# Low parts of weights on VectorE, mixing between the gates' pairs, LayerNorm as paced work: a change to a two-branch decoder kernel

## The chip, the core and the metric

The kernel runs on one core of one Trainium2 chip. The metric is the device time of one execution in microseconds (us). TensorE multiplies (PE in the rows, its weight loads PEld), VectorE (DVE) and ScalarE (ACT) do elementwise work, GpSimd (POOL) issues the accumulating DMAs, SyncE (SP) issues most loads and stores.

## The reference, cut to what matters

One layer over 1040 prompt positions (16 learned ones ahead of 1024) and 64 sample positions (8 sequences of 8, with states), D = 1024, all float32:

```
h = rmsnorm(x); z = h @ w_in            # seven column groups of 1024
u = a_val * sigmoid(a_gate)             # GLU
c = causal_depthwise_conv(u, width 31) + b
c = silu(layernorm(c)) * silu(a_silu);  br_a = c @ w_conv_out
pooled = trailing_mean(p_in, 2/4/8/16 by channel group) - p_in
q = (pooled per group @ w_pool_mix) * pool_scale * silu(p_silu)
br_b = q @ w_pool_out
y = rmsnorm(x + (sigmoid(g_a)*br_a + sigmoid(g_b)*br_b) @ w_out)
```

The last 30 values of `u` and the last 15 of `p_in` are returned as new states.

## The kernel before

Channels lie on the 128 partitions, positions on the free axis, in two halves `h` of 552 columns (8 learned, 512 prompt, 32 sample) or 544 without the learned ones. Every float32 operand of a product is split into a high part (rounded to the type that TensorE takes) and a low part (the rest), and a product is three passes: high x high, high x low, low x high (`gemm`). Two helpers make the parts. `split` casts on ScalarE and subtracts on VectorE:

```python
act.copy(dst_h, src)
dve.tensor_tensor(dst_l, src, dst_h.bitcast(F32), ALU.subtract)
```

`split_dma` casts on ScalarE, writes the negated high part with `act.mul` into the low tile, and lets an accumulating DMA of GpSimd's queue add the source.

The stages, in order of emission:

1. *Plain products* of p0 to p5 (pool inputs) with x before its normalisation (`plain`, `keep_raw`), while the root of the mean square is made. Then VectorE normalises x (L332) and `split_x` makes the operands hx.
2. *Blocks*: 18 products of 96 matmuls (p6, p7, then gate g and value v of each of eight chunks of the GLU). Weights are loaded two blocks ahead and split one block ahead (`Block.split`, by default `split_dma`). A v block ends in the GLU, whose result goes to DRAM (d_e, d_es) and comes back as the convolution's input.
3. *Pairs*: 16 pairs of column blocks (q, b, a, s: the four gates), each by seven products of 24 matmuls instead of eight (`seven`), with sums of weights on VectorE and low parts mostly by `split_dma`. All gates go to DRAM.
4. *Mixing*: the pooled operand, split when it was made (`pool_work`, `out`), is loaded as two parts and multiplied by w_pool_mix, gated (L840) and split into the slots q.
5. *Branch B's projection* (`ppo`, 8 x 2 halves of 48 matmuls). Beside it, after the first half of blocks written out by hand, LayerNorm: the mean from a sum that accumulating DMAs made, the squares, the root (`inv_root`), and `branch_a`, which makes the operands cx.
6. *Branch A's projection* (`pco`, of the same size) with the merge, then the final projection (`pwo`) and norm.

VectorE's convolution (31 taps of 1024 columns per chunk and four sample steps) and the pooling are queued work: `push` puts lists of (cost, step) into `todo`, and `fill(until)` emits steps while the planner's account of VectorE stays under the one of TensorE. `step(us)` adds to TensorE's account and runs what `defer` has put off by a number of steps; `spend(n)` charges VectorE with 0.22 + n/960 us for work that is emitted outside the queue. Every engine and queue runs its instructions in the order of emission. Tiles come from rings: 35 slots of 4.4 KB a partition, ten half raw weights, six half operands, eight z tiles (half a row of positions), four PSUM tiles of two banks. A tile is given back when nothing refers to it any more, and whoever takes the next one waits for that.

Of the kernel before, what the change touches and what calls it, by code (L numbers as in the profile page):

```python
# [14 lines left out]
P = 128  # L15
# [28 lines left out]
NSLOT, NWS, NOP, NZ = 35, 10, 6, 8  # L44
# [4 lines left out]
BLOCKS = "p6 p7 " + " ".join(f"g{i} v{i}" for i in range(8))  # L49
# [19 lines left out]
def hybrid_trunk_kernel(  # L69
# [40 lines left out]
    ones32 = const.tile([P, P], F32, name="ones32")  # L110
# [67 lines left out]
    def totals(s, n, name):  # L178
        hl = [slot(f"sum{x}_{name}", (2, n), F32R) for x in "hl"]
        split(hl[0], hl[1], s)  # L180
        out = slot(f"total_{name}", (2, n))
# [149 lines left out]
    for k in range(NK):  # L331
        dve.scalar_tensor_tensor(xs[k], xs[k], col(OFF_NG, k), rms, ALU.mult, ALU.mult)  # L332
        split_x(0, (k,), split)
    plain1(1)
    plain1(2)
    keep_raw(1, 1, outs[1])
    split_x(1, (0, 1), split)
    plain1(3)
    keep_raw(2, 1, outs[2])
    split_x(1, (2, 3), split)  # L340
    plain1(4)
    keep_raw(3, 1, outs[3])
# [94 lines left out]
    def seven(w, units, put):  # L437
# [14 lines left out]
        y = bank2(f"py_{name}")  # L452
        act.copy(y[:, :, :n], x[:, :, :n])
        yield
        v = bank2(f"pv_{name}")
        product_of(v, "q3", "T3", True, False)
        yield
        fill(clock["pe"])
# [25 lines left out]
    d_gate, d_sga, d_sgb, d_sa, d_c, d_tb = (  # L484
        dram.tile([NK, P, 2, H2], F32, name=f"d_{x}") for x in ("gate", "sga", "sgb", "sa", "c", "tb")
    )
    d_pool = dram.tile([NK, P, 2, 2, H2], F32, name="d_pool")
# [14 lines left out]
    def pool_load(j):  # L502
        if j < NK:
            lraw[j] = [half(f"lraw{j}{h}") for h in range(2)]
            for h in range(2):
                sp.dma_start(out=lraw[j][h], in_=d_raw[j][:, h])

    def pool_work(j):
# [3 lines left out]
        def start():  # L512
# [3 lines left out]
            sp.dma_start(out=es[:, :, :PB], in_=spool[j])  # L516
            for h in range(2):
# [11 lines left out]
            defer(2, lambda: sp.dma_start(out=o_ps[j], in_=es[:, :, DS:]))  # L529
# [10 lines left out]
        def last():  # L540
            e, es, s, ss = cur
            dve.scalar_tensor_tensor(s[:, META:], s[:, META:], 1.0 / w, e[:, META:], ALU.mult, ALU.subtract)  # L542
            dve.scalar_tensor_tensor(ss[:, :, PB:], ss[:, :, PB:], 1.0 / w, es[:, :, PB:], ALU.mult, ALU.subtract)

        def out(h):
            s, ss = cur[2:]
            o = slot(f"poolop{j}{h}", (2, H2), F32R)
            b = slice(h * DB // 2, (h + 1) * DB // 2)
            split_dma(o[:, 0, :HP], o[:, 1, :HP], s[:, META + h * HP : META + (h + 1) * HP])
            split(v3(o[:, 0, HP:], DS), v3(o[:, 1, HP:], DS), ss[:, b, PB:])  # L550
            defer(3, lambda: sp.dma_start(out=d_pool[j][:, h], in_=o.bitcast(F32)))
# [7 lines left out]
        for h in range(2):  # L559
            work.append((0.25, lambda h=h: out(h)))  # L560
# [5 lines left out]
    def gate_pair(i, base, name, func, dst):  # L566
        def put(b, h, z):
            o = z
            if not b:
                o = half2(f"z{name}{i}{b}{h}", H2)  # L570
            act.activation(o, z, func)
            act.dma_start(out=dst[2 * i + b][:, h], in_=flat(o))

        return [(w_in[base + 2 * i], w_in[base + 2 * i + 1], f"{name}{i}", UNITS2, put)]
# [3 lines left out]
    d_e = dram.tile([NK, P, TP], F32, name="d_e")  # L578
    d_es = dram.tile([NK, P, DB, DS], F32, name="d_es")


    class Conv:
        fetched = []

        def __init__(self, i):
            self.i = i
            work = [(t_op(SEQ) if k else 0.75, lambda k=k: self.taps(k)) for k in range(CW)]
            work += [(1.5, lambda b=b: self.sample(b)) for b in range(0, DB, 2)]
# [11 lines left out]
        def fetch(self):  # L600
            i = self.i
            e = self.e = slot(f"ce{i}", (CB + TP,))
            es = self.es = st.tile([P, DB, ES], F32, tag="ces", name=f"ces{i}", bufs=2)
            pool.memset(e[:, :CB], 0.0)
            sp.dma_start(out=e[:, CB:], in_=d_e[i])
            sp.dma_start(out=es[:, :, :CB], in_=sconv[i])
            sp.dma_start(out=es[:, :, CB:], in_=d_es[i])
            defer(3, lambda: sp.dma_start(out=o_cp[i], in_=e[:, TP : TP + CB]))
            defer(3, lambda: sp.dma_start(out=o_cs[i], in_=es[:, :, DS:]))
# [28 lines left out]
        def store(self):  # L638
            Conv.fetched.remove(self)
            Conv.more()  # L640
            defer(2, self.put)

        def put(self):
            sp.dma_start(out=d_c[self.i], in_=self.c)
            if not csum:
                csum.append(dram.tile([P, 2, H2], F32, name="d_csum"))
                sp.dma_start(out=csum[0], in_=self.c)
            else:
                pool.dma_start(out=csum[0], in_=self.c, accum_op=ALU.add)
# [6 lines left out]
    def put_block(kind, i, h, ps):  # L656
# [7 lines left out]
        else:  # L664
            z = sg.pop(h)
            dve.tensor_tensor(v3(z, HT // 2), ps, v3(z, HT // 2), ALU.mult)
            spend(HT)
            m, p, s = parts4(z)

            def out():  # L670
                sp.dma_start(out=d_e[i][:, META + h * HP : META + (h + 1) * HP], in_=p)
                sp.dma_start(out=d_e[i][:, h * HM : (h + 1) * HM], in_=m)
                sp.dma_start(out=d_es[i][:, h * DB // 2 : (h + 1) * DB // 2], in_=s)

            defer(1, out)
# [6 lines left out]
    ops[0].split()  # L682
# [7 lines left out]
    def make_t(k, how):  # L690
# [13 lines left out]
        "q": lambda i: gate_pair(i, PSG, "q", AF.Silu, d_gate),  # L704
# [35 lines left out]
    pooled, wm = {}, {}  # L740

    def load_pooled(j):
        pooled[j] = [slot(f"lp{j}{h}", (2, H2), F32R) for h in range(2)]
        for h in range(2):
            sp.dma_start(out=pooled[j][h].bitcast(F32), in_=d_pool[j][:, h])

    def load_mix(g):
        raw = half_raw(f"mraw{g}")
        sp.dma_start(out=raw.rearrange("p k c -> p (k c)"), in_=w_mix[g].rearrange("p k c -> p (k c)"))
        wm[g] = op_tile(f"m{g}", (2, 2, 2 * P))  # L750
        split(wm[g][:, 0], wm[g][:, 1], raw.rearrange("p (k a) c -> p k (a c)", k=2))
# [3 lines left out]
    lgate = {}  # L755

    def load_gate(j):
        lgate[j] = [fetch_half(d_gate[j], h, f"lg{j}") for h in range(2)]

# [3 lines left out]
    for n, (kind, i) in enumerate(blocks):  # L763
# [3 lines left out]
        if n + 1 < len(blocks):  # L767
            ops[n + 1].split()
# [5 lines left out]
        for h in (0, 1) if left > 1 else (1, 0):  # L774
# [4 lines left out]
            if n == 0 and h == 0:  # L779
                keep_raw(5, 1, outs[5])  # L780
# [12 lines left out]
    clock["t"] = 0  # L793
    cur = pairs[0][1]
    next(cur), next(cur), next(cur)
    after = iter(())
    for n in range(len(pairs)):
        nxt = pairs[n + 1][1] if n + 1 < len(pairs) else None
        next(after, None)
        next(cur)  # L800
        if nxt:
            next(nxt)
        else:
            load_mix(0)
            load_gate(0)
            load_pooled(0)
            load_pooled(1)
        next(cur)
        if nxt:
            next(nxt)  # L810
        next(cur)
        if nxt:
            next(nxt)
        after, cur = cur, nxt
    next(after, None)
    fill()

    load_pooled(2)
    load_gate(1)
    q = []  # L820
    for j in range(NK):
        if j + 3 < NK:
            load_pooled(j + 3)
        if j + 2 < NK:
            load_gate(j + 2)
        if j % 2 == 0 and j < 6:
            load_mix(j // 2 + 1)
        if j == 4:
            po[0].load()
            po[0].split()  # L830
        if j == 6:
            po[1].load()
        g, i = j // 2, j % 2
        q.append([])
        for h in range(2):
            ps = gemm_half(
                f"pmix{j}", lambda k, s: wm[g][:, s, k, i * P : (i + 1) * P], [pooled[2 * g], pooled[2 * g + 1]], h, 2
            )
            z = lgate[j][h]
            dve.scalar_tensor_tensor(of_half(z), ps, col(OFF_PS, j), of_half(z), ALU.mult, ALU.mult)  # L840
            q[j].append(operand(f"q{j}{h}", z, split))
            step(1.5)


    conv = [slot(f"lc{i}", (2, H2)) for i in range(NK)]
    lcsum = slot("lcsum", (2, H2))
    sp.dma_start(out=lcsum, in_=csum[0])
    cx = []
    lsa = {}

    def load_sa(i):
        lsa[i] = [fetch_half(d_sa[i], h, f"lsa{i}") for h in range(2)]

    def branch_a(i, how):
        cx.append([])
        dve.tensor_tensor(conv[i], conv[i], rstd, ALU.mult)
        act.activation(conv[i], conv[i], AF.Silu, bias=col(OFF_LB, i), scale=col(OFF_LG, i))
        for h in range(2):
            dve.tensor_tensor(conv[i][:, h], conv[i][:, h], lsa[i][h], ALU.mult)
            cx[i].append(operand(f"cx{i}{h}", conv[i][:, h], how))  # L860

    for d in range(NK):
        (po + co)[d + 2].load()
        lb = [fetch_half(d_sgb[d], h, f"lb{d}") for h in range(2)]
        if d == 0:
            for i in range(NK):
                sp.dma_start(out=conv[i], in_=d_c[i])
        (po + co)[d + 1].split()
        if d == 1:
# [250 lines left out]
```

## Time and profile before

| | us |
|---|---|
| median of three runs (1117.55 to 1118.63) | 1117.84 |
| the profiled execution | 1117.58 |
| its span, first to last instruction | 1115.8 |
| TensorE busy | 990.3 |
| VectorE busy | 731.9 |
| ScalarE busy | 469.1 |
| GpSimd busy | 174.4 |

Busy time is that of the profiled execution. Matmuls overlap, so their durations add up to more than the time in which they run; the distance between two starts is what one costs. PEclk is the clock granted to TensorE as a share of full speed; its two levels are 2.4 and 1.2 GHz.

### The profile page before, as it was taken

To read this page: it belongs to the slowest core of one execution; us is meant where nothing else is said; L and a number is where in the kernel's file an instruction comes from. 1 tells how busy PE (TensorE), PEld (TensorE's weight loads), DVE (VectorE), ACT (ScalarE), POOL (GpSimd) and SP (SyncE) were. 2 spreads that over 40 slices of the span, in tenths; PEclk is the share of its full clock that TensorE was granted. 3 is DMA by queue.
4 is the path that set the end of the run, shared out by engine and by line. 5 is a ranking of instruction groups with operands and counts; after the bars stand their busy time and mean duration, and the time that the engine had idled before them with its cause. 6 is when DMAs were issued, how large, how long until landed. Compare 5 with 4: busy or idle time off the path is not lost. (4 is left out here: it accounts for less than half of the span.)

```text
span 1115.8 us, 18229 instructions
## 1 busy us (share of the span) xinstructions
PE 990.3 (89%) x7176; PEld 962.1 (86%) x7176; DVE 731.9 (66%) x945; ACT 469.1 (42%) x791; POOL 174.4 (16%) x211
## 2 busy tenths in 40 slices
PE   9978885789999899999999999759967649999997
PEld 9978885789999899999999999758967649998885
DVE  7473542698998999999898998354434443355333
ACT  7635432313325665655455555234236452225111
POOL 0001211111213222322222232001011121000000
PEclk9999998789999999999999999979998969999999
DMA  9217999996559797989879796999346569544222
GB/s 318 73 48 165 198 214 201 205 233 162 119 143 204 171 234 185 225 200 207 197 176 239 180 224 145 309 343 320 101 107 184 161 187 279 153 155 150 77 94 95
DMA packets 144805, 205.94 MB, mean 185 GB/s; under 512 B 59216, under 2 KB 60624, under 8 KB 144720
## 3 DMA queue, kind: packets, MB, share of 16 engines
q1 hardware_dynamic: 104832, 128.42, 38.6%
q0 software_dynamic: 28368, 54.01, 28.0%
q10 hardware_dynamic: 11520, 22.35, 6.0%
q8 instruction: 56, 0.92, 0.3%
q14 instruction: 29, 0.24, 0.1%
HBM read 99.37 MB, written 55.27 MB: 139 GB/s over the span
## 5 line engine op out<-in xcount | busy, mean ns | idle before, releaser
L621 DVE SCALAR_TENSOR_TENSOR c<-ce,pv,c 128x1024 f32<-128x1024 f32 x240 | 307.9, 1283 | 5.9
L149 PE MATMUL pv<-hx,w_v 128*128 128x276 f32 x768 | 105.1, 299 | 20.7 <-DMA w_v<-raw_v 20.7
L149 PEld LDWEIGHTS pv<-hx,w_v 128*128 128x128 f32 x768 | 103.2, 197 | 21.8 <-DMA w_v<-raw_v 21.8
L149 PE MATMUL pco<-cx,w_co 128*128 128x272 f32 x768 | 101.6, 295 | 22.4 <-DMA w_co<-raw_co 11.4
L149 PEld LDWEIGHTS pco<-cx,w_co 128*128 128x128 f32 x768 | 100.1, 194 | 23.8 <-DMA w_co<-raw_co 12.1
L149 PE MATMUL pg<-hx,w_g 128*128 128x276 f32 x768 | 104.5, 298 | 14.2 <-DMA w_g<-raw_g 14.2
L149 PEld LDWEIGHTS pg<-hx,w_g 128*128 128x128 f32 x768 | 103.0, 197 | 14.9 <-DMA w_g<-raw_g 14.9
L149 PE MATMUL ppo<-q,w_po 128*128 128x272 f32 x768 | 100.0, 293 | 6.4 <-DMA w_po<-raw_po 6.0
L149 PEld LDWEIGHTS ppo<-q,w_po 128*128 128x128 f32 x768 | 99.2, 192 | 7.2 <-DMA w_po<-raw_po 6.4
L993 PE MATMUL pwo<-wo,mx 128*128 128x512 f32 x336 | 79.3, 394 | 0.0
L993 PEld LDWEIGHTS pwo<-wo,mx 128*128 128x128 f32 x336 | 63.1, 188 | 14.8
L149 PE MATMUL pp<-xg,wh_p 128*128 128x276 f32 x384 | 66.8, 296 | 7.8 <-ACT rawp L259 7.7
L149 PEld LDWEIGHTS pp<-xg,wh_p 128*128 128x128 f32 x384 | 56.5, 194 | 8.7 <-ACT rawp L259 7.9
L149 PE MATMUL pmix<-lp,m 128*128 128x272 f32 x192 | 31.5, 329 | 16.7 <-DVE lg L840 10.6
L878 DVE TENSOR_TENSOR lb<-ppo,lb 128x544 f32<-128x544 f32 x16 | 11.5, 722 | 52.0 <-DMA lb<-d_sgb 40.2
L149 PEld LDWEIGHTS pmix<-lp,m 128*128 128x128 f32 x192 | 29.6, 225 | 18.5 <-issue 10.0
L149 PE MATMUL pp<-xg,wl_p 128*128 128x276 f32 x192 | 40.7, 294 | 0.0
L663 ACT ACTIVATE zg<-pg 128x552 f32<-128x552 f32 x16 | 9.9, 628 | 68.8 <-PE pg L149 63.3
L119 ACT CAST mx<-lga 128x544 fp32r<-128x544 f32 x16 | 10.3, 646 | 61.0 <-DVE lga L954 61.0
L1012 DVE TENSOR_TENSOR xr<-pwo,xr 128x1024 f32<-128x1024 f32 (+1 forms) x9 | 10.0, 1106 | 39.4 <-DMA xr<-in_xres 24.8
L124 ACT CAST poolop<-pw 128x512 fp32r<-128x512 f32 x16 | 9.9, 618 | 60.8 <-DVE pw L542 33.1
L975 ACT ACTIVATE sq<-xr 128x1024 f32<-128x1024 f32 (+1 forms) x9 | 8.7, 965 | 63.5 <-DVE xr L1012 63.5
(328 smaller groups left out, 1918.2 us busy)
## 6 DMA issues: line engine op xcount, KB each, us to landing
d_pool<-poolop SPq DMA_DIRECT2D x16, 544.0 KB, 7.9
lp<-d_pool SPq DMA_DIRECT2D x16, 544.0 KB, 7.6
lraw<-d_raw SPq DMA_DIRECT2D x16, 276.0 KB, 7.5
d_c<-c SPq DMA_DIRECT2D x8, 544.0 KB, 5.8
lg<-d_gate SPq DMA_DIRECT2D x16, 272.0 KB, 6.1
lb<-d_sgb SPq DMA_DIRECT2D x16, 272.0 KB, 6.4
lc<-d_c SPq DMA_DIRECT2D x8, 544.0 KB, 9.1
d_tb<-lb SPq DMA_DIRECT2D x16, 272.0 KB, 2.2
```

Of the source, the lines that this page charges most:

```text
L119: act.copy(dst_h, src)
L124: act.copy(dst_h, src)
L149: pe.matmul(out[:, u, : hi - lo], w(k, a), xs(k, b)[:, lo:hi], start=first and k == ks[0] and i == 0, stop=last and k == ks[-1] and i == 2 ...
L621: dve.scalar_tensor_tensor(c, s, wk, c, ALU.mult, ALU.add)
L663: act.activation(v3(sg[h], HT // 2), ps, AF.Sigmoid)
L878: dve.tensor_tensor(of_half(lb[h]), ps, of_half(lb[h]), ALU.mult)
L975: act.activation(sq[:rows, c], xr[:, c], AF.Square, accum_out=a1 if ns[0] else a0)
L993: pe.matmul(ps[:, n - ns[0]], x(k), wo[k][n][w], start=(k == 0 and s == 0), stop=(k == NK - 1 and s == len(passes) - 1),)
L1012: dve.tensor_tensor(v3(xr[:, c], 512), ps[:, : len(ns)], v3(xr[:, c], 512), ALU.add)
```

## The change

- `Block.split` is called with `split` everywhere: the low parts of plain weights (blocks, both projections) are made on VectorE, and the planner is charged for them.
- The order of blocks is now g0 v0 p6 p7 g1 v1 ..., and the normalisation is emitted in pieces between the plain products, behind the copies of their results.
- The pooled operand goes to DRAM unsplit (8 stores). The mixing is cut into quarters (12 matmuls each) that are emitted between the products of the pair after the q gate in question; that gate stays in SBUF; the mixed q goes to DRAM and is reloaded and split in the last pair.
- LayerNorm becomes queued work behind the convolution and is paid out in branch B's projection. A chunk of the convolution that ends after the pairs stays in SBUF instead of going through DRAM. All of cx is split on VectorE.
- States are loaded into whole tiles and joined with the new values by GpSimd copies; the states that are returned are gathered by GpSimd before they are stored. The zeros ahead of the convolution's input are in DRAM. 34 slots instead of 35, eleven z tiles instead of eight.
- In a pair, the copy of the first product into a second PSUM tile moves behind the second product.

```diff
-NSLOT, NWS, NOP, NZ = 35, 10, 6, 8
+NSLOT, NWS, NOP, NZ = 34, 10, 6, 11
...
+    def norm_x(ks):
+        for k in ks:
+            dve.scalar_tensor_tensor(xs[k], xs[k], col(OFF_NG, k), rms, ALU.mult, ALU.mult)
+            split_x(0, (k,), split)
     plain1(1)
+    keep_raw(1, 1, outs[1])
     plain1(2)
+    norm_x((0,))
+    keep_raw(2, 1, outs[2])
+    norm_x((1, 2, 3))
...
         if n + 1 < len(blocks):
-            ops[n + 1].split()
+            ops[n + 1].split(split)
+            spend(512, 2)
...
+            pool.tensor_copy(es[:, :, :PB], stage)
+            pool.tensor_copy(stage, es[:, :, DS:])
...
+        def join(self):
+            i, state = self.i, self.state
+            es = self.es = st.tile([P, DB, ES], F32, tag="ces", name=f"ces{i}", bufs=1)
+            pool.tensor_copy(es[:, :, :CB], state)
+            pool.tensor_copy(es[:, :, CB:], self.new)
+            pool.tensor_copy(state, es[:, :, DS:])
...
+        def gate(self, j, h, ps):
+            z = pool_gate.pop((j, h))
+            dve.scalar_tensor_tensor(of_half(z), ps, col(OFF_PS, j), of_half(z), ALU.mult, ALU.mult)
+            spend(H2)
+            defer(1, lambda: sp.dma_start(out=d_q[j][:, h], in_=z))
...
+        if mix:
+            mix.split(0)
+            mix.split_w()
+            mix.load(1)
...
         next(after, None)
         next(cur)
-        if nxt:
-            next(nxt)
+        if mix:
+            mix.gate(*mix.part(0, 0))
+        next(nxt, None)
+        if mix:
+            mix.gate(*mix.part(0, 1))
+            mix.split(1)
+        next(cur)
+        if mix:
+            mix.gate(*mix.part(1, 0))
...
+    finish_a = [(5.0, root)] + [(5.2, lambda i=i: branch_a(i)) for i in range(NK)]
+    squares_ = [(2.7, lambda i=i: centre(i)) for i in range(NK + 1)]
+    squares_.append((1.3, lambda: begin_totals(0, "var", finish_a)))
+    push([(1.3, lambda i=i: sum_rest(i)) for i in range(NK)] + [(1.3, lambda: begin_totals("sum", "mean", squares_))])
     for d in range(NK):
...
-            step(6.0)
+            step(2 * T_PRODUCT)
+            if d == 0:
+                load_conv(h * 4, h * 4 + 4)
+                if h:
+                    load_sum()
+            else:
+                fill(clock["pe"])
+    while todo or due:
+        fill()
+        step(0.0)
```

## Rows read from the trace of the kernel before

**Rows 1.** Stretches: busy time of each engine (instructions), granted clock, DMA share, GB/s.

```profile
74.70:90.81 16.11, 7.80 (x48) 7.58 (x48) 10.84 (x14) 9.40 (x17) 0.00 (x0) 0.79 0.30 105
...
121.00:362.90 241.90, 207.03 (x1538) 205.23 (x1537) 178.64 (x236) 76.76 (x139) 48.52 (x59) 0.94 0.89 187
362.90:713.40 350.50, 342.53 (x2690) 341.00 (x2689) 315.64 (x366) 195.32 (x325) 88.54 (x104) 0.99 0.85 201
713.40:762.00 48.60, 31.50 (x194) 29.50 (x192) 20.52 (x29) 12.56 (x21) 1.72 (x2) 0.79 0.98 352
762.00:893.80 131.80, 103.73 (x784) 102.03 (x784) 55.34 (x61) 55.90 (x74) 16.64 (x20) 0.92 0.58 166
893.80:1011.40 117.60, 101.57 (x769) 100.37 (x770) 53.59 (x76) 38.04 (x61) 11.16 (x13) 0.92 0.67 189
1011.40:1115.80 104.40, 96.40 (x416) 77.76 (x415) 42.47 (x87) 22.58 (x70) 0.00 (x0) 0.99 0.30 102
```

**Rows 2.** Groups of TensorE's lines: count, busy, mean ns, idle before and its releaser.

```profile
L149 PE MATMUL pv<-hx,w_v 128*128 128x276 f32 x768 | 105.1, 299 | 20.7 <-DMA w_v<-raw_v 20.7
L149 PE MATMUL pg<-hx,w_g 128*128 128x276 f32 x768 | 104.5, 298 | 14.2 <-DMA w_g<-raw_g 14.2
```

**Rows 3.** Timeline of TensorE: start, length, instructions, idle before and releaser.

```profile
82.28 1.29 PE L149 MATMUL pp<-xg,wh_p 128*128 128x276 f32 x4 [7.67 <-ACT rawp L259]
...
95.47 4.72 PE L149 MATMUL pp<-hx,w_p 128*128 128x276 f32 x23 [3.89 <-DMA w_p<-raw_p]
...
288.33 11.88 PE L149 MATMUL pg<-hx,w_g 128*128 128x276 f32 x92
...
532.24 3.03 PE L149 MATMUL px_b<-tT,woq_b 128*128 128x272 f32 x13 [2.06 <-DMA woq_b<-q_b]
...
700.38 3.19 PE L149 MATMUL py_s<-hx,wob_s 128*128 128x272 f32 x24
703.40 3.16 PE L149 MATMUL px_s<-tT,woq_s 128*128 128x272 f32 x24
...
904.15 6.03 PE L149 MATMUL pco<-cx,w_co 128*128 128x272 f32 x32 [9.04 <-DMA w_co<-raw_co]
```

**Rows 4.** Timeline of VectorE and ScalarE where the normalisation ends.

```profile
81.74 0.73 DVE L120 TENSOR_TENSOR hx<-x,hx 128x552 fp32r<-128x552 f32 x1 [0.72 <-ACT hx L119]
...
82.62 1.21 ACT L119 CAST hx<-x 128x552 fp32r<-128x552 f32 x2 [0.40 <-ACT rawp L259]
```

**Rows 5.** Timeline of VectorE, taps in a block and one step of LayerNorm.

```profile
298.47 9.21 DVE L621 SCALAR_TENSOR_TENSOR c<-ce,pv,c 128x1024 f32<-128x1024 f32 x7
...
899.97 1.28 DVE L856 TENSOR_TENSOR lc<-lc,ir_c 128x1088 f32<-128x1088 f32 x1
902.61 0.73 DVE L859 TENSOR_TENSOR lc<-lc,lsa 128x544 f32<-128x544 f32 x1 [1.36 <-ACT lc L857]
904.05 0.72 DVE L120 TENSOR_TENSOR cx<-lc,cx 128x544 fp32r<-128x544 f32 x1 [0.71 <-ACT cx L119]
...
906.76 1.28 DVE L856 TENSOR_TENSOR lc<-lc,ir_c 128x1088 f32<-128x1088 f32 x1
```

**Rows 6.** Timeline of ScalarE and VectorE: first and last step of the root.

```profile
840.54 1.08 ACT L119 CAST sumh_v<-vsum 128x1088 fp32r<-128x1088 f32 x1
...
853.84 1.29 DVE L200 TENSOR_TENSOR ir_c<-ir_c,it_c 128x1088 f32<-128x1088 f32 x1
```

**Rows 7.** Groups of VectorE's lines: low part of weights, gate of the mixing.

```profile
L840 DVE SCALAR_TENSOR_TENSOR lg<-pmix,pv,lg 128x544 f32<-128x544 f32 x16 | 12.5, 778 | 0.0
...
L120 DVE TENSOR_TENSOR w_co<-raw_co,w_co 128x512 fp32r<-128x512 f32 x6 | 3.9, 684 | 0.0
```

**Rows 8.** The tile ce: min/median/max ns, first and last start.

```profile
L621 DVE SCALAR_TENSOR_TENSOR c<-ce,pv,c x240: 1274/1285/1290, 221.5 to 698.5; 128x1024 f32<-128x1024 f32 x120
L604 POOL MEMSET ce<- x8: 124/458/946, 169.7 to 582.7; 128x30 f32 x8
```

**Rows 9.** DMA issues: count, KB each, median us to landing.

```profile
lp<-d_pool SPq DMA_DIRECT2D x16, 544.0 KB, 7.6
```

More of the change, by code (lines that the diff above doesn't have):

```diff
@@ L457, in seven @@
         yield
+        y = bank2(f"py_{name}")
+        act.copy(y[:, :, :n], x[:, :, :n])
         fill(clock["pe"])
@@ L515, in start @@
             cur.extend((e, es, e, es))
-            sp.dma_start(out=es[:, :, :PB], in_=spool[j])
+            stage = lraw[j][2]
             for h in range(2):
@@ L541, in last @@
             e, es, s, ss = cur
[L542 to L551, printed above, removed]
+            o = slot(f"pool{j}", (2, H2))
+            dve.scalar_tensor_tensor(
+                o[:, :, :HP], v3(s[:, META:], HP), 1.0 / w, v3(e[:, META:], HP), ALU.mult, ALU.subtract
+            )
+            for h in range(2):
+                c = slice(h * DB // 2, (h + 1) * DB // 2)
+                dve.scalar_tensor_tensor(
+                    v3(o[:, h, HP:], DS), ss[:, c, PB:], 1.0 / w, es[:, c, PB:], ALU.mult, ALU.subtract
+                )
+            defer(1, lambda: sp.dma_start(out=d_pool[j], in_=o))
         work = [(0.0, lambda: pool_load(j + 1)), (2 * (t_op(HP) + 0.5), start)]
@@ L793, in hybrid_trunk_kernel, with load_q, split_q @@
     clock["t"] = 0
+    names = ORDER.split()
+    first_q = names.index("q0")
+    q, qraw = [], {}
+    def load_q(j):
+        qraw[j] = [fetch_half(d_q[j], h, f"lq{j}") for h in range(2)]
+    def split_q(j):
+        q.append([operand(f"q{j}{h}", z, split) for h, z in enumerate(qraw.pop(j))])
+        spend(H2, 2)
     cur = pairs[0][1]
-    next(cur), next(cur), next(cur)
+    next(cur), next(cur)
     after = iter(())
+    mix = None
     for n in range(len(pairs)):
-        nxt = pairs[n + 1][1] if n + 1 < len(pairs) else None
+        nxt = pairs[n + 1][1] if n + 1 < len(pairs) else iter(())
+        if mix:
+            mix.split(0)
+            mix.split_w()
+            mix.load(1)
+        if n + 1 == len(pairs):
+            for j, t in enumerate((1, 1, 2, 2, 3, 4, 5, 5)):
+                if j > 1:
+                    defer(t - 2, lambda j=j: load_q(j)) if t > 2 else load_q(j)
+                defer(t, lambda j=j: split_q(j))
+            defer(1, po[0].load)
+            defer(3, po[1].load)
+            defer(5, lambda: po[0].split(split))
@@ L808, in hybrid_trunk_kernel @@
+        if n + 2 == len(pairs):
+            load_q(0)
+            load_q(1)
         next(cur)
[L809 to L813, printed above, removed]
+        tail = mix.part(1, 1) if mix else None
+        next(nxt, None)
+        if tail:
+            mix.gate(*tail)
+        mix = coming
         after, cur = cur, nxt
     next(after, None)
[L816 to L842, printed above, removed]
@@ L845, in hybrid_trunk_kernel, with load_conv @@
[L845 to L849, printed above, removed]
-    def load_sa(i):
-        lsa[i] = [fetch_half(d_sa[i], h, f"lsa{i}") for h in range(2)]
-    def branch_a(i, how):
+    Conv.keep = True
+    conv, cx, lsa, norm = {}, [], {}, {}
+    def load_sa(i):
+        if i < NK:
+            lsa[i] = [fetch_half(d_sa[i], h, f"lsa{i}") for h in range(2)]
+    def load_conv(lo, hi):
+        for i in range(lo, hi):
+            if getattr(chunks[i], "stored", False):
+                conv[i] = slot(f"lc{i}", (2, H2))
+                sp.dma_start(out=conv[i], in_=d_c[i])
@@ new lines, in load_sum, with sum_rest, begin_totals, run @@
+    def load_sum():
+        norm["sum"] = slot("lcsum", (2, H2))
+        sp.dma_start(out=norm["sum"], in_=csum[0])
+    def sum_rest(i):
+        if not chunks[i].stored:
+            conv[i] = chunks[i].c
+            dve.tensor_tensor(norm["sum"], norm["sum"], conv[i], ALU.add)
+    def begin_totals(key, name, work):
+        parts_ = total_parts(norm[key], H2, name)
+        def run():
+            norm[name] = total_products(parts_, H2, name)
+            push(work)
+        defer(1, run)
@@ new lines, in centre, with root, branch_a @@
+    def centre(i):
+        if i < NK:
+            dve.tensor_tensor(conv[i], conv[i], norm["mean"], ALU.subtract)
+            norm[i] = slot("vsum" if i == 0 else f"csq{i}", (2, H2))
+            act.activation(norm[i], conv[i], AF.Square)
+        if i > 1:
+            dve.tensor_tensor(norm[0], norm[0], norm.pop(i - 1), ALU.add)
+    def root():
+        norm["rstd"] = inv_root(norm["var"], H2, LN_EPS, "c")
+        load_sa(0)
+        load_sa(1)
+    def branch_a(i):
+        load_sa(i + 2)
@@ L864, in hybrid_trunk_kernel @@
         lb = [fetch_half(d_sgb[d], h, f"lb{d}") for h in range(2)]
[L865 to L869, printed above, removed]
-            mean = totals(lcsum, H2, "m")
-        if d == 5:
-            rstd = inv_root(totals(vsum, H2, "v"), H2, LN_EPS, "c")
-        if d >= 5:
-            for i in ((0, 1), (2, 3, 4), (5, 6, 7))[d - 5]:
-                load_sa(i)
+        (po + co)[d + 1].split(split)
+        spend(512, 2)
         for h in range(2):
```

197 lines of the change are left out of this document (111 added, 86 removed).

## The prediction

> **What bounds the kernel now.** I read the stretches first [rows 1]: TensorE is busy in every stage and VectorE in the first five, so what counts is TensorE's idle and half-speed time, stage by stage. At the full clock a block's matmul takes (11.88 - 0.28) / 91 = 0.1275 us, so a block of 96 takes 12.24 us; a product of 24 in a pair takes 703.40 - 700.38 = 3.02 us, 0.1258 us a matmul [rows 3]. Against that, 121.0 to 362.9 us holds 16 blocks, 195.8 us of work in 241.9: 46.1 us lost. The pairs hold 16 x 7 x 3.02 = 338.2 in 350.5: 12.3 lost. The mixing is 192 matmuls, 24.1 in 48.6: 24.5 lost. Branch B's projection is 768, 96.6 in 131.8 up to the first matmul of A's: 35 lost. A's own is 96.6 in 117.6: 21 lost. The final projection has TensorE busy throughout. Second, who ends the idle time: in the blocks the low weights that come by accumulating DMA, 20.7 and 14.2 us [rows 2]; before the sixth plain product the PSUM copy that ScalarE holds behind VectorE's normalisation, 7.67, and then again a low weight, 3.89 [rows 3]. The 11 us that idle and product sum leave open in the blocks are the lower clock, 0.94 in that stretch [rows 1]; after a gap of 9.04 us, 32 matmuls took 6.03 us instead of 31 x 0.126 + 0.28 = 4.2, so a long gap costs 1.9 us on top, and after 2.06 us of idleness 13 took 3.03 instead of 1.8 [rows 3].
>
> **Start.** The normalisation stays one chain on VectorE and ends at about 82.5 [rows 4]; moving it behind the PSUM copies lets TensorE run through all plain products to 74.7 + 6.1 = 80.8. The first block now needs, on ScalarE from 81.7 us on, eight casts of the other half and two of weights at 0.6 (1.21 for two), and the last PSUM copy with its DMA issue (0.6 + 0.4) [rows 4]: 88.7; with one VectorE subtraction of 0.69 [rows 7] the block starts at 89.5. Before, p6 started at 90.8 and stood another 3.89.
>
> **Blocks.** Each of 36 half blocks of weights loses a ScalarE multiplication and an accumulating DMA and gets a VectorE subtraction of 0.684 us [rows 7]: 25 us on VectorE. It lies under the products: a block's two are emitted one block (12.24 us) ahead, and the planner now charges them (1.51 a block), so convolution taps move out by as much. Without that cover each would stand 0.7 us before its block, 25 in all. Pool inputs and conv states come through whole staging tiles that GpSimd joins, the split of the pooled operand leaves this stage, and 16 stores of 544 KB become 8: fewer bytes on DMA engines that are 0.89 busy [rows 1]. I take the stalls away but for 4 us (0 to 25, half the 46.1), and 1.9 for the clock after the 8.7 us gap: 89.5 + 18 x 12.24 + 1.9 + 4 = 315.7, against 362.9.
>
> **Pairs with mixing.** The pairs keep their 350.5. The mixing adds 24.1 of product. Its VectorE work per pair (four splits, the weights, four gates) is charged at 7.05. SyncE loads the pooled halves one pair ahead or before the second half (7.6 us to landing [rows 9]); behind them on SyncE stand the weights of the pairs, with eight products of lead; three more z buffers make room. ScalarE's queue loses the 16 stores of the pooled gates, which now stay in SBUF until their quarter has been gated; SyncE gets 16 stores and 16 reloads of q (272 KB) for as many reloads of gates, the reloads in the last pair, behind that pair's own weights. One wait is new. The second gate cannot run before its quarter is done; behind it on VectorE stand the other half's splits (2 x 0.73 and a wait of 0.71 for the cast [rows 5]), two taps at 1.31 (9.21 / 7) and the combination c4, which product d needs: 0.78 + 2.2 + 2.6 + 0.7 = 6.3 us, while TensorE has one product and one quarter, 4.5, until then. So 1.8 us in each of four pairs; between 0 and 1.8 + 1.3 for the clock, so 0 to 12; I take 8. End: 315.7 + 350.5 + 24.1 + 8 = 698.3.
>
> **Branch B's projection.** Its weights are split on VectorE, its gates' buffers are no longer eight, and the total for the variance no longer stands in it: 96.6 + 1 for the total of the sums + 5 (0 to 10) for the last splits of q, which are waiting for their reloads, = 102.6. End at 800.9.
>
> **LayerNorm, where I expect the loss.** The planner pays work out only while its VectorE account is below its TensorE account, so I added its own costs up (an operation of n elements is 0.22 + n/960). To the end of the pairs TensorE's account is 18 x 12 + 16 x 21 + 16 x 1.5 = 576. The queue holds 8 x 45.4 of conv and 66.9 of pool, 430. Charged beside the queue: 17 x 1.51 for weights, 16 x 0.795 for values, 16 x 0.795 for make_t, 16 x 5.34 in the pairs, 4 x 7.05 for mixing, 12.6 for q: 177. So 576 - 177 = 399 are paid, and, step by step, 30 of conv 7 stay over. (The same count for the kernel before has the queue empty 8 us before the pairs end; its last tap starts at 698.5 of 713.4 [rows 8].) Branch B adds 96, of which its own splits and gates take 24.6 and an overdraft 3: 68.5. Queued first are 30.4 of conv, 10.4 for sum_rest (eight entries, though one chunk alone needs it), 1.3, 24.3 for the squares, 1.3: 67.7. That fills it. The root and all eight `branch_a` steps, 46.6 by the planner, come after the last product of B, in the loop that drains the queue, and the first product of A needs all eight.
>
> Their real length: from the last gate of B 0.72 + 1.29 and a handover, 2.1; from the cast of the squares' sum to the root 840.54 to 855.13 = 14.6 [rows 6]; then a branch whose two halves are both split on VectorE has a pitch of 906.76 - 899.97 = 6.79, not 5.2, because VectorE waits for ScalarE's silu (1.36) and casts (0.71 each) in it [rows 5]. Before, half of the branches left the low part to DMA and all lay in B's last three blocks. The first half of the eighth is ready 4.8 into it: 2.1 + 14.6 + 7 x 6.79 + 4.8 = 69.0 after B. TensorE does seven eighths of A's first half meanwhile (5.3), then 96.6 - 5.3 = 91.3, and 1.9 for the clock: 162.2 from B's end to A's end. Ends: 155 (a branch of 5.9, if casts overlap) and 168 (one more such wait of 0.71 in each of the eight).
>
> The conv's last chunk stays in SBUF (one reload of 544 KB less, hidden anyway). A's weights on VectorE cost 16 x 0.684, under 96 us of product in which VectorE is half idle [rows 1].
>
> **Sum.** 800.9 + 162.2 + 104.4 for the untouched end [rows 1] = 1067.5 of span. The profiled execution took 1117.58 with a span of 1115.8, so 1.8 lie around it; the median of the runs, 1117.84, is 0.26 above it. Predicted: 1069 us.
>
> **Rivals.**
> - *LayerNorm does fit* (the change does what its name says): if VectorE's account has 47 us more than I count, root and branches lie under B's products, and A's projection takes 96.6 instead of 162.2: 1004. For it: VectorE is under half busy there now. Against: the sums above. 0.07.
> - *GpSimd's joins hold VectorE up.* Taps run 1.274 to 1.290 us, almost without spread, while GpSimd's only work on SBUF data is a fill of 124 to 946 ns, median 458 [rows 8]. The change adds 40 copies that read SBUF (16 for pool, 24 for conv). If each keeps the next tap waiting for a fill's 0.46, VectorE, which has no slack in blocks and pairs, hands 18 us to TensorE: 1087. For it: the planner does not charge them; against: the fills show nothing. 0.13. The Trainium skill states the rule behind this (SBUF — State Buffer, "Who interferes with whom"): a VectorE operation with two SBUF inputs and a GpSimd operation that reads SBUF share a read port, and the second to issue is blocked until the first is done. By that rule a tap waits for a whole copy or the copy for a tap, so up to those 18 us; fills only write, so no run yet shows it.
> - *Loads, not accumulations, set the blocks.* Half of the blocks' 46.1 us stays, 23 instead of 4: 1088. For it: DMA share 0.89 there; against: the rows name the accumulation. 0.14.
> - *Slower.* The pooled halves wait for z buffers and land only after the pair wants them: 8 loads of 7.6 us exposed whole [rows 9] are 61 us, 1130. It decides from 49 / 8 = 6.1 us exposed a load on. For it: up to 12 buffers are wanted of 11; against: two were loaded a product and two quarters ahead. 0.05.
> - *The forecast*, 1052 to 1084 by its own unknowns (blocks, c4, branch pitch): 0.61.
>
> The range 1040 to 1099 takes in the second and third rival, and leaves out the first and the fourth and their neighbours. Faster by over 0.2% (2.2 us, about what this measurement tells from no change): 0.94, the same 0.01, slower 0.05.
>
> **What would show it.** Right: no accumulating DMA ahead of w_g and w_v, TensorE unbroken over the 18 blocks (some 222 us); mixing quarters inside the first pairs of the next gate with idle steps of about 2 us ahead of d; one gap of some 65 to 70 us between B's and A's projections in which TensorE does only small groups about 6.8 us apart, with VectorE waiting on casts. Wrong: branches under B's products; taps longer than 1.29 us beside GpSimd copies; idle time in the blocks that ends with a load of raw weights; or idle time in the pairs that ends with a pooled load.

## The result, and the profile after

The changed kernel takes 1076.67 us (median; 1076.08 to 1078.14), the kernel before took 1117.69 beside it: ratio 0.9644, 95% interval 0.9614 to 0.9674. Predicted were 1069, and 1040 to 1099. A second measurement gave 1076.16 against 1107.84 (0.9697, 0.9673 to 0.9721): the changed kernel repeats within 0.1%, while the kernel before differs by 0.9% between the two. So the experiments below are also read in us against 1076.2 to 1076.7.

The profiled execution took 1076.53 with a span of 1074.7. Its stretches (time, then TensorE, its weight loads, VectorE, ScalarE and GpSimd busy, granted clock, DMA share, GB/s), to be held against [rows 1]: the handover to the blocks, the 18 blocks, pairs with mixing, branch B's projection, from there to the end of A's, the final projection.

```profile
80.90:88.20 7.30, 0.26 (x3) 0.04 (x2) 5.93 (x10) 6.29 (x12) 0.00 (x0) 0.87 0.38 121
88.20:310.07 221.87, 221.86 (x1728) 221.53 (x1729) 186.75 (x271) 46.15 (x79) 29.67 (x32) 0.99 0.46 138
310.07:701.30 391.23, 370.25 (x2882) 365.49 (x2880) 343.11 (x401) 213.89 (x359) 101.94 (x117) 0.98 0.81 204
701.30:810.40 109.10, 100.03 (x778) 99.52 (x777) 72.29 (x85) 23.84 (x33) 0.00 (x0) 0.95 0.46 160
810.40:969.50 159.10, 109.69 (x777) 104.92 (x776) 84.40 (x114) 51.21 (x71) 0.00 (x0) 0.79 0.41 125
969.50:1074.70 105.20, 96.32 (x418) 77.90 (x416) 42.64 (x88) 22.57 (x70) 0.00 (x0) 0.97 0.30 102
```

All 18 blocks now run without a break, at a granted clock of 0.99 where it was 0.94. From 90.81 to 362.90 the same 1728 matmuls took 272.1 us before: 50.2 are won there. Pairs and mixing, 399.1 before, take 391.2: 7.9 won. The last stretch is as it was; from the end of the mixing to the end of A's projection it is 268.2 against 249.4: 18.8 lost. The groups that answer to [rows 2], and those of the two projections (count, busy, mean ns, idle before and its releaser):

```profile
L149 PE MATMUL pv<-hx,w_v 128*128 128x276 f32 x768 | 98.8, 289 | 0.0
L149 PE MATMUL pg<-hx,w_g 128*128 128x276 f32 x768 | 101.3, 293 | 7.1 <-ACT w_g L119 7.0
L149 PE MATMUL ppo<-q,w_po 128*128 128x272 f32 x768 | 99.2, 292 | 9.1 <-DVE w_po L120 8.2
L149 PE MATMUL pco<-cx,w_co 128*128 128x272 f32 x768 | 108.5, 304 | 47.5 <-ACT cx L119 47.5
```

The 35 us that the blocks waited for accumulating DMAs are gone; 47.5 us of waiting for branch A's normalised halves have come in.

**The tail behind B.** TensorE's timeline, the first three of eight groups (start, length, instructions, idle before and releaser):

```profile
827.87 2.03 PE L149 MATMUL pco<-cx,w_co 128*128 128x272 f32 x6 [14.19 <-ACT cx L119]
834.67 2.03 PE L149 MATMUL pco<-cx,w_co 128*128 128x272 f32 x6 [4.77 <-ACT cx L119]
841.47 2.03 PE L149 MATMUL pco<-cx,w_co 128*128 128x272 f32 x6 [4.76 <-ACT cx L119]
```

Groups of six matmuls 6.80 us apart; eight branches lie behind B. Why 6.80 is seen on VectorE, one branch:

```profile
833.21 0.73 DVE L982 TENSOR_TENSOR lc<-lc,lsa 128x544 f32<-128x544 f32 x1 [1.36 <-ACT lc L980]
834.65 0.73 DVE L120 TENSOR_TENSOR cx<-lc,cx 128x544 fp32r<-128x544 f32 x1 [0.71 <-ACT cx L119]
835.29 0.72 DVE L982 TENSOR_TENSOR lc<-lc,lsa 128x544 f32<-128x544 f32 x1
836.72 0.73 DVE L120 TENSOR_TENSOR cx<-lc,cx 128x544 fp32r<-128x544 f32 x1 [0.71 <-ACT cx L119]
837.36 1.28 DVE L979 TENSOR_TENSOR lc<-lc,ir_c 128x1088 f32<-128x1088 f32 x1
```

VectorE and ScalarE hand one tile to and fro: 2.78 us of each 6.80 VectorE waits.

**A wait in the pairs.** Two rows of TensorE's timeline; then ScalarE ahead of the first of them, ScalarE ahead of the second, and VectorE ahead of the second:

```profile
321.46 4.95 PE L149 MATMUL px_q<-tT,woq_q 128*128 128x272 f32 x24 [4.87 <-ACT py_q L467]
...
409.37 2.41 PE L149 MATMUL px_q<-tT,woq_q 128*128 128x272 f32 x9 [4.76 <-ACT py_q L467]
```

```profile
320.27 0.63 ACT L125 ACTIVATE woa_q<-woa_q 128x512 fp32r<-128x512 f32 x1
320.80 0.61 ACT L467 COPY py_q<-px_q 128x544 f32<-128x544 f32 x1
```

```profile
403.18 0.65 ACT L119 CAST px<-lp 128x544 fp32r<-128x544 f32 x1 [1.75 <-DMA lp<-d_pool]
404.06 0.65 ACT L119 CAST px<-lp 128x544 fp32r<-128x544 f32 x1 [0.23 <-DMA lp<-d_pool]
406.14 0.62 ACT L119 CAST m<-mraw 128x512 fp32r<-128x512 f32 x1 [1.44 <-DMA mraw<-in_w_mix]
408.15 0.66 ACT L583 ACTIVATE c_q<-c_q 128x544 f32<-128x544 f32 x1 [1.39 <-DVE c_q L489]
408.71 0.61 ACT L467 COPY py_q<-px_q 128x544 f32<-128x544 f32 x1
```

```profile
406.79 0.69 DVE L120 TENSOR_TENSOR m<-mraw,m 128x512 fp32r<-128x512 f32 x1 [1.33 <-ACT m L119]
407.40 0.72 DVE L489 SCALAR_TENSOR_TENSOR c_q<-pv_q,c_q 128x544 f32<-128x544 f32 x1
```

TensorE wants y, the copy of a pair's first product in a second PSUM tile. The copy takes 0.61 us, but at 409 us ScalarE's queue holds it behind three casts of the mixing, each of which waits for a load, and an activation that waits for VectorE's combination, itself behind the mixing's split. Seven waits end with this copy (4.87, 2.33, 1.57, 4.76, 1.74, 0.81, 0.98), 17.1 us in all. The first, 4.87, is of another kind: it lies in the first pair, where no cast of the mixing stands ahead of the copy, only splits of the pairs' weights. The other six make 12.2.

**A wait in B's projection.** TensorE, then ScalarE, then SyncE's queue:

```profile
747.52 12.76 PE L149 MATMUL ppo<-q,w_po 128*128 128x272 f32 x84 [7.83 <-DVE w_po L120]
```

```profile
746.60 1.22 ACT L119 CAST w_po<-raw_po 128x512 fp32r<-128x512 f32 x2 [18.08 <-DMA raw_po<-in_w_po]
```

```profile
741.74 0.32 SPq L999 DMA_DIRECT2D d_tb<-lb  x1
742.15 0.88 SPq L385 DMA_DIRECT2D raw_po<-in_w_po  x2
```

The load of the weights is issued late because the store `d_tb` stands ahead of it on SyncE, and that store waits for a gate that VectorE reached only after the planned work which had not been paid out in the first of the loop's eight column blocks: nine taps, 11.84 us, stand directly ahead of that gate.

### The profile page after: what moved, and what is told of

The parts are those of the page before. It is cut to its first block, busy times and chain, and to the rows that moved or that the text cites. A ratio compares the mean times of both kernels' runs of the same rounds, so it can differ in the third digit from the quotient of the medians.

```text
span 1074.7 us, 18019 instructions
## 1 busy us (share of the span) xinstructions
PE 977.6 (91%) x7176; PEld 947.4 (88%) x7176; DVE 784.9 (73%) x1024; ACT 412.1 (38%) x689; POOL 133.1 (12%) x157
## 2 busy tenths in 40 slices
DMA packets 96150, 172.92 MB, mean 161 GB/s; under 512 B 20929, under 2 KB 24385, under 8 KB 96065
## 4 chain that ended last, share of the span: by engine, by line
PE 67%; DVE 13%; ACT 9%; issue 4%; DMA 4%; SPq 1%; ACTq 1%; POOL 0%; DVEq 0%; POOLq 0%
PE pg L149 9%; PE pco L149 9%; PE pv L149 9%; PE ppo L149 7%; PE pp L149 6%; PE px_s L149 5%; PE px_a L149 5%; PE px_b L149 5%; PE pwo L1108 4%; DVE c L663 3%; PE px_q L149 2%; DMA xr<-in_xres 2%; PE pmix L149 1%; PE py_a L149 1%; PE py_b L149 1%
## 5 line engine op out<-in xcount | busy, mean ns | idle before, releaser
L149 PE MATMUL pco<-cx,w_co 128*128 128x272 f32 x768 | 108.5, 304 | 47.5 <-ACT cx L119 47.5
L149 PEld LDWEIGHTS pco<-cx,w_co 128*128 128x128 f32 x768 | 103.9, 200 | 52.1 <-ACT cx L119 50.1
L149 PE MATMUL pg<-hx,w_g 128*128 128x276 f32 x768 | 101.3, 293 | 7.1 <-ACT w_g L119 7.0
L149 PEld LDWEIGHTS pg<-hx,w_g 128*128 128x128 f32 x768 | 100.1, 192 | 7.6 <-ACT w_g L119 7.3
L149 PE MATMUL pv<-hx,w_v 128*128 128x276 f32 x768 | 98.8, 289 | 0.0
L149 PEld LDWEIGHTS pv<-hx,w_v 128*128 128x128 f32 x768 | 98.0, 188 | 0.0
L149 PE MATMUL pp<-xg,wh_p 128*128 128x276 f32 x384 | 65.7, 291 | 0.7 <-DVE xg L218 0.3
L149 PE MATMUL px_q<-tT,woq_q 128*128 128x272 f32 x192 | 29.4, 316 | 13.5 <-ACT py_q L467 13.5
L149 PEld LDWEIGHTS px_q<-tT,woq_q 128*128 128x128 f32 x192 | 28.2, 215 | 14.4 <-ACT py_q L467 14.4
L1068 DVE TENSOR_TENSOR lga<-pco,lga 128x544 f32<-128x544 f32 x16 | 11.6, 724 | 33.8 <-PE pco L149 33.8
L997 DVE TENSOR_TENSOR lb<-ppo,lb 128x544 f32<-128x544 f32 x16 | 11.5, 721 | 32.3 <-DMA lb<-d_sgb 17.5
```

What stands on the lines that cost most here:

```text
L149: pe.matmul(out[:, u, : hi - lo], w(k, a), xs(k, b)[:, lo:hi], start=first and k == ks[0] and i == 0, stop=last and k == ks[-1] and i == 2 ...
L997: dve.tensor_tensor(of_half(lb[h]), ps, of_half(lb[h]), ALU.mult)
L1068: dve.tensor_tensor(of_half(ga), ps, of_half(ga), ALU.mult)
```

## The experiments

Unless said otherwise, each is the changed kernel with the edit shown. `...` marks what is left out.

**1. Branch A's normalisations staggered.** Branch i's scaling and silu are issued ahead of the products and casts of branch i - 1, both halves of a step together.

```
-            cx[i].append(operand(f"cx{i}{h}", conv[i][:, h], split))
+        if i > 0:
+            j = i - 1
...
+            for h in range(2):
+                act.copy(o[h][:, 0], conv[j][:, h])
+            for h in range(2):
+                dve.tensor_tensor(o[h][:, 1], conv[j][:, h], o[h][:, 0].bitcast(F32), ALU.subtract)
```

> The steps of branch_a are staggered: a chunk's scaling and silu are issued one step ahead of the multiplications by the gate, both halves' multiplications before the casts and both casts before the subtractions. Same work, same planner costs. Theory (the pitch of 6.8 us between the small groups of A's first product is VectorE waiting for ScalarE, 1.36 + 2 x 0.71 a chunk, on 4.1 us of its own work): pitch 4.0 to 4.3 us, the gap between B's and A's projections 18 us shorter, about 1059 us. Rival (VectorE's or ScalarE's own throughput sets the pitch): pitch stays above 6 us, 1075 to 1078 us.

Measured: 1058.03 us, ratio 0.9523 (0.9479 to 0.9567). TensorE's timeline behind B, the first three of eight groups, of this kernel:

```profile
831.13 2.03 PE L149 MATMUL pco<-cx,w_co 128*128 128x272 f32 x6 [14.48 <-ACT cx L987]
835.58 2.04 PE L149 MATMUL pco<-cx,w_co 128*128 128x272 f32 x6 [2.42 <-ACT cx L987]
840.04 2.04 PE L149 MATMUL pco<-cx,w_co 128*128 128x272 f32 x6 [2.42 <-ACT cx L987]
```

A branch is 4.46 us instead of 6.80 (4.0 to 4.3 were expected), and B's end to A's end 141.7 instead of 159.1. The tail was the handover between two engines, eight times, as the forecast had it.

**2. The copy of y first.** In each pair the generator of the gate is stepped once before the mixing's casts are issued, so that ScalarE's copy (L467) stands ahead of them.

```
+        yield
...
+        next(cur)
```

> In every pair but the first the copy of the first product into its second PSUM tile is issued ahead of the mixing's splits and of the last combination (c2) of the pair before. Theory (TensorE's idle time in the pairs, 17 us that end with this copy, comes from where it stands in ScalarE's queue, behind an activation that waits for c2 on VectorE): the waits on the copy go except the first of 4.9 us, pairs and mixing take 376 to 380 us instead of 391, about 1063 us. Rival (the pooled operands or VectorE are late whatever the order): the same idle time shows up ahead of the next product or quarter, 1073 to 1077 us.

Measured: 1061.15 us, ratio 0.9552 (0.9503 to 0.96). The window of pairs and mixing of this kernel:

```profile
309.10:685.00 375.90, 365.21 (x2882) 362.59 (x2880) 342.60 (x402) 214.79 (x359) 102.20 (x117) 1.00 0.84 212
```

375.9 instead of 391.2, with VectorE's and ScalarE's work the same: the order on one queue cost 15.3 us. Of the seven waits on the copy the first, now 4.88, stays. Three waits of 0.68 to 1.18 ahead of quarters of the mixing are new. TensorE's busy time is 5.0 us shorter, at a granted clock of 1.00 instead of 0.98.

**3. Planned work in the first of B's eight column blocks too** (the expectation of experiment 7 calls it the first quarter).

```
-            else:
-                fill(clock["pe"])
+            fill(clock["pe"])
```

> The planner also pays out queued work in the first block of B's projection. Theory (the 7.8 us stall in B's projection is the lump of some 16 us of taps emitted at once in the second block, behind which a gate, its store and the load of raw weights queue): the stall goes, about 1068 us. Rival (that load is late because eight reloads of the convolution crowd the DMA engines): the stall stays within 2 us of 7.8, 1075 to 1078 us.

Measured: 1066.24 us, ratio 0.9597 (0.9553 to 0.9641). All idle time before the products of B's projection, of this kernel (releaser: us, times), then the window from B's first product to its last:

```profile
  ACT w_po L119: 0.9, 1
  DVE w_po L120: 0.3, 1
```

```profile
705.49:803.94 98.45, 98.07 (x777) 97.53 (x777) 71.27 (x83) 22.96 (x31) 0.00 (x0) 1.00 0.50 175
```

The stall of 7.83 is gone, and the stretch is granted a clock of 1.00 instead of 0.95.

**4. The blocks' low parts through DRAM again**, the other parts of the change kept.

```
-            ops[n + 1].split(split)
-            spend(512, 2)
+            ops[n + 1].split(split_dma)
```

> One part undone: in the blocks alone the low parts of weights are made by ScalarE and accumulating DMAs again, and the planner isn't charged for them. Theory (these accumulations stalled TensorE in the blocks): idle time of 20 to 35 us that ends with them comes back, blocks of 245 to 260 us instead of 222, in part given back behind B, since LayerNorm starts some 26 us earlier: 1065 to 1085 us. Rival (other relief of the DMA engines, unsplit pooled operands and whole pieces of states, took the stalls away): blocks of 222 to 228 us, and half of the branches fit under B's projection, 1035 to 1045 us.

Measured: 1047.38 us, ratio 0.9435 (0.9387 to 0.9482). The windows of the 18 blocks, and from B's end to A's end, of this kernel:

```profile
87.70:316.40 228.70, 224.45 (x1728) 223.68 (x1729) 192.35 (x258) 67.58 (x113) 60.73 (x70) 0.98 0.69 177
...
817.30:940.00 122.70, 102.45 (x770) 100.23 (x769) 65.64 (x93) 33.85 (x54) 0.00 (x0) 0.89 0.43 137
```

With the accumulating DMAs back, the blocks still lose only 4.2 us of idle time to them (34.9 before, for w_v and w_g alone). VectorE is spared the subtractions and the planner their charge, and the root and four branches come in under B's products: the tail is 122.7 instead of 159.1. The low parts on VectorE cost this kernel 29 us (23 by the ratios): 6.8 won in the blocks, 36.4 lost in the tail.

**5. The low parts on VectorE alone**, in the kernel before.

```
-        def split(self, how=split_dma):
+        def split(self, how=None):
+            how = how or split
...
+            spend(512, 2)
```

> The kernel before with one part of the change alone: every plain weight of the blocks gets its low parts by a subtraction on VectorE (about 0.78 us each by the row of w_g) instead of through DRAM and an accumulating transfer; the pooled operand is still split with GpSimd's tap tile and the small pieces as before. Theory (the late accumulations alone stalled the blocks): the blocks last 222 to 228 us instead of 242, and the whole is 14 to 20 us shorter, ratio 0.982 to 0.988. Rival (the transfers are crowded by the other parts' traffic too, so that the raw loads come late as the accumulations did, and VectorE's added 22 us of work is then paid later): the blocks stay above 235 us, the ratio is 0.99 to 1.02.

Measured: 1092.89 us, ratio 0.983 (0.9789 to 0.9871). The expectation set bounds for 18 blocks beside the 242 us of 16; the 18 were 272.1. They take 235.7 here (the first row); the mixing is the second:

```profile
91.20:326.90 235.70, 224.51 (x1727) 223.84 (x1728) 183.79 (x276) 68.00 (x128) 23.21 (x29) 0.97 0.72 166
...
681.50:741.90 60.40, 31.01 (x194) 30.07 (x193) 41.44 (x55) 11.74 (x19) 0.87 (x1) 0.72 0.78 268
```

36.4 us are won in the blocks. 11.8 are given back in the mixing, where VectorE has 41.4 us of work instead of 20.5 [rows 1]: eleven taps of the convolution, 14.48 us, now stand ahead of the mixing's first gate. What is left of the stalls, in the timeline of this kernel:

```profile
145.70 0.34 DVE L538 TENSOR_TENSOR pws<-pes 128x176 f32<-128x176 f32 x1 [6.81 <-DMA pes<-in_spool]
145.96 1.29 DVE L120 TENSOR_TENSOR w_g<-raw_g,w_g 128x512 fp32r<-128x512 f32 x2
...
146.70 6.56 PE L149 MATMUL pg<-hx,w_g 128*128 128x276 f32 x31 [5.45 <-DVE w_g L120]
```

The row names VectorE's subtraction as the releaser, but VectorE stood 6.81 us before a small pooled piece that a DMA brought late; the subtraction was queued behind it. So transfers other than the accumulations were late too. Each theory has half of this run: the ratio is in the first one's range, the blocks' 235.7 (above 235) and the late loads are the rival's.

**6. GpSimd's copies twice.** Each joining and gathering copy is issued two times.

> The changed kernel with every joining and gathering copy of GpSimd made twice. Theory (beside VectorE's taps it is GpSimd's copies that are stretched, and the taps keep their 1.27 us to within a tenth): within 3 us of the changed kernel, ratio 0.962 to 0.967, taps of 1.26 to 1.43 us. Rival (the copies hold the taps up): taps with a mean above 1.35 us and 10 to 18 us more, ratio 0.973 to 0.98.

Measured: 1077.64 us, ratio 0.9683 (0.9649 to 0.9717); 1.0 to 1.5 us more than the changed kernel. The tile ce and GpSimd's copies, of the changed kernel (min/median/max ns):

```profile
L663 DVE SCALAR_TENSOR_TENSOR c<-ce,pv,c x240: 1268/1285/1431, 146.1 to 754.4; 128x1024 f32<-128x1024 f32 x120
...
L648 POOL COPY ces<-cst x8: 388/886/1683, 148.7 to 687.1; 128x240 f32<-128x240 f32 x8
L649 POOL COPY ces<-csn x8: 237/1230/1992, 149.0 to 687.8; 128x64 f32<-128x64 f32 x8
```

and of the kernel with the copies doubled:

```profile
L667 DVE SCALAR_TENSOR_TENSOR c<-ce,pv,c x240: 1269/1285/1465, 145.8 to 756.8; 128x1024 f32<-128x1024 f32 x120
...
L652 POOL COPY ces<-csn x16: 236/1226/1993, 148.8 to 691.6; 128x64 f32<-128x64 f32 x16
```

GpSimd is 25.2 us busier (158.3 against 133.1), VectorE 2.9 (787.8 against 784.9); the taps' median stays at 1285 ns. The ratio lies between the two ranges expected, 0.962 to 0.967 and 0.973 to 0.98; the time and the taps are the theory's. The copies do not hold VectorE up.

**7 and 8. The four edits together** (1 to 4), and with B's projection weights through DRAM as well. Both, and 9 and 10 after them, also lower two of the planner's costs, which their expectations do not name: a step of branch A is charged 4.5 instead of 5.2, and `sum_rest` of a stored chunk nothing instead of 1.3.

```
+    finish_a = [(5.0, root)] + [(4.5, lambda i=i: branch_a(i)) for i in range(NK + 1)]
...
+    push([(0.0 if getattr(chunks[i], "stored", False) else 1.3, lambda i=i: sum_rest(i)) for i in range(NK)] ...
```

> The changed kernel with the four edits that each shortened it put together: branch A's normalisations staggered, the copy of y issued ahead of the mixing's casts, planned work in the first quarter of branch B's projection too, and the blocks' low parts through DRAM again. If the gains add, each by its own ratio against the changed kernel's 0.9644: 13.4 + 10.2 + 5.2 + 23.2 = 52 us, about 1025 us, ratio 0.917. If they overlap: fewer normalisations are left behind branch B when the blocks' work goes to the transfers, so staggering is worth about half, and 1030 to 1036 us, ratio 0.922 to 0.928, comes out.

> As the four edits together, with branch B's projection weights taking their low parts through DRAM as well, so that VectorE is spared about 16 subtractions, some 11 us, in that stage. If VectorE's work there decides what is left for the tail: 5 to 9 us less than the four edits together. Rival (the accumulations of that stage come after the product wants them, as w_po did): products of the projection idle on a transfer, and the time is the same or up to 10 us longer.

Measured: 1019.95 us, ratio 0.9163 (0.9132 to 0.9195), and 1017.15, 0.9144 (0.9114 to 0.9174). Against the changed kernel the first wins 56.5 us, where the single gains in us (18.4, 15.3, 10.2 and 29.1, from 1076.4) make 73. By ratios, as the expectation counts, the singles make 52 and the whole 53 to 54, and 0.9163 is close to the 0.917 of gains that add. But the ratios lean on a kernel before that differed from one measurement to the next, and the spans of the profiled executions do not: the singles shorten 1074.7 by 15.1, 18.1, 7.4 and 29.4, 70 in all, and the four together by 56.4. So the gains overlap. A's products in the first wait for a normalised half only three times (2.52, 3.05 and 0.75 us), so little of the tail was left to stagger; how much of that the lower planner costs did, no run shows. The second is no different from the first within the intervals: its A projection runs unbroken in 96 us, but B's waits 5.2 us for `w_po` that accumulating DMAs bring. Both have a wait that the changed kernel does not have, for the reload of the sum (in the first, VectorE's idle time in us and how often; then TensorE's row):

```profile
  DMA lcsum<-d_csum: 8.3, 1
```

```profile
721.00 0.59 PE L193 MATMUL pt_mean<-sumh_mean,ones 128*128 128x272 f32 x1 [7.15 <-ACT sumh_mean L119]
```

**9, 10 and 11. The reload of the sum ahead of the eight of the convolution**, in both, beside the changed kernel.

```
+                if not h:
+                    load_sum()
                 load_conv(h * 4, h * 4 + 4)
-                if h:
-                    load_sum()
```

> The four edits together, and the reload of the sum issued ahead of the eight reloads of the convolution instead of behind them. In the four edits' run TensorE stood 7.15 us before the total of the sums, and VectorE waited for that reload. Theory (the queue of reloads is what the total waits for): the stall is gone and the whole 5 to 8 us shorter than the four edits together (ratio 0.909 to 0.912). Rival (the time is only moved: VectorE then comes no earlier to the squares and the tail behind branch B grows by as much): within 2 us, ratio 0.915 to 0.918.

> The same edit of the reload of the sum in the kernel whose projection weights of branch B come through DRAM, where the stall was 8.30 us: 6 to 9 us shorter than that one (ratio 0.907 to 0.909), or within 2 us by the rival (0.913 to 0.916).

> The changed kernel itself once more, beside these two, so that their gains are read against it on the same chip: ratio 0.961 to 0.968.

Measured: 1010.51 us, 0.9108 (0.9083 to 0.9132); 1012.46, 0.9135 (0.9109 to 0.9161); 1076.16, 0.9697 (0.9673 to 0.9721). In the first the stall is gone and the time 9.4 us shorter (6.1 by the ratios; 5 to 8 were expected), as the theory had it; B's and A's stretches of its trace:

```profile
694.48:794.12 99.64, 99.17 (x784) 98.51 (x784) 69.17 (x87) 43.07 (x54) 0.00 (x0) 1.00 0.58 202
794.12:902.86 108.74, 101.81 (x769) 99.96 (x769) 59.74 (x87) 29.04 (x49) 0.00 (x0) 0.94 0.47 154
```

The second missed its expectation. It is 4.7 us shorter (1.0 by the ratios) instead of 6 to 9, and its ratio lies in the rival's range, 0.913 to 0.916. The stall is gone there too, but the waits for such a `w_po` grew from 5.2 to 8.3 us (releaser: us, times):

```profile
  DMA w_po<-raw_po: 8.3, 3
```

The low parts that gain from a transfer are the blocks', not B's. The third missed 0.961 to 0.968, though its time repeats: the kernel before was faster beside it. Experiment 9 is the best version: 65.7 to 66.2 us below the changed kernel.

## Why the prediction was right, point by point

It was 7.7 us short of 1076.67. Start, blocks and tail together took 8.7 us less than their terms, the pairs, B's projection and the end 15.9 more. That the whole came out within 1% is in part luck: these errors cancel. One reading at its head is too wide: by [rows 1] VectorE is busy for 0.67 to 0.90 of the first three stretches and for 0.42 of the fourth and fifth. Nothing in the sum rests on it.

- **Start.** The first block at 89.5: measured 88.2, with one gap of 7.04 behind ScalarE's cast of `w_g`.
- **Blocks.** 226.2 us with 4 of stalls: 221.9 with none. The size was right, its reason only half. The prediction credited the end of the stalls to the low parts on VectorE and kept "loads, not accumulations" as a rival. The four cases (18 blocks; whole ratio) are: before 272.1; low parts alone 235.7, 0.983; the other parts alone 228.7, 0.9435; both 221.9, 0.9644 (0.9697 in the second measurement). Either removes most of the stalls, so an accumulating DMA is not late as such: in the third case all of the blocks' are back and cost 4.2 us. What both lighten is the traffic. DMA share per 100 GB/s falls from 0.48 (0.89 at 184 before) to 0.43, 0.39 and 0.33 in the same order. The page counts the packets, here of the kernel with the low parts alone and then of the one with the other parts alone:

```profile
DMA packets 135877, 189.69 MB, mean 175 GB/s; under 512 B 58224, under 2 KB 59632, under 8 KB 135792
```

```profile
DMA packets 101044, 181.83 MB, mean 174 GB/s; under 512 B 21472, under 2 KB 24928, under 8 KB 100960
```

  Between these two lie some 37,000 packets under 512 B (before had 59,216, the changed kernel has 20,929). The Trainium skill (DMA: Bandwidth & Descriptors, "Specifications") gives 512 B as the smallest transfer at full rate. With these packets gone the share per 100 GB/s falls from 0.48 to 0.39 and from 0.43 to 0.33, which agrees, but the pooled operand's split goes in the same two steps. The queue of the accumulating DMAs itself moved 16.7 MB in the blocks before, 7.0 with the low parts alone, 12.1 with the other parts alone and 2.5 with both, so a limit of that queue is a third candidate, though the late pooled piece of experiment 5 did not come through it. No run here takes one of the three alone; which of them relieved the transfers stays open.
- **Pairs with mixing.** 382.6 predicted, 391.2 measured. The wait ahead of the combination, priced at 8, is 0.79 + 0.32 + 0.78 = 1.9. Not priced: the copy of y in ScalarE's queue, 17.1. Experiment 2 shows it for the 12.2 behind the mixing; the 4.87 of the first pair stay in it. The prediction looked at what stands behind the waiting gate on VectorE, and not at what the mixing's casts hold up on ScalarE.
- **Branch B's projection.** 102.6 predicted, 109.1 measured: the unpriced 7.83 behind the late load, shown by experiment 3. The 5 priced for the last splits of q did not come: only 1.2 us of waiting, for `w_po`, stand at its start.
- **B's end to A's end.** 162.2 predicted, 159.1 measured, by the mechanism forecast: root and eight branches behind B, pitch 6.80 against 6.79. The eighth's first half is ready 65.0 after B's end instead of 69.0: the first branch's comes at 17.5, where the terms make 21.5. That the planner's account is the cause fits experiment 4, which gets four branches in; its edit takes both VectorE's work and the charge away, and VectorE is busy for 72.29 of B's 109.1 us, so it had time for more than the planner paid out.
- **End.** 104.4, measured 105.2.
- **Rivals.** LayerNorm did not fit. GpSimd's copies do not lengthen the taps (experiment 6). No wait in the pairs ends with a pooled load at TensorE, but at 409 us the casts that hold up y wait for loads of the mixing by 0.23 to 1.75 us.

## What to carry to other kernels

When a transfer is late, ask whether that transfer is slow or all are: a cure by other work on a busy engine is paid again where that engine's queue ends, and here the lighter transfers alone were worth 29 us more than both together. An instruction that takes half a microsecond and frees TensorE goes to the head of its queue, ahead of everything that waits for a load. A chain that two engines hand to and fro is staggered by one step.

## What was not expected of the hardware

GpSimd's copies beside VectorE's work are stretched up to eightfold (128x64: 237 to 1992 ns; spans on GpSimd are rough in the profile), while the taps' median does not move and their longest goes from 1290 to 1431 ns. The 237 ns are the one such copy that ran while VectorE stood idle (at 235.8 us); three with taps alone beside them took 1.23 us each, about one tap. The Trainium skill (SBUF — State Buffer, "Who interferes with whom") says that the second to issue is blocked; the rows agree for the copies, and a tap lost at most 0.15 us. Here GpSimd pays nearly alone.
